# First MLP product token-major, convolution by accumulating transfers, gated result transposed: a two-layer encoder on one core

## The chip, the core and the metric

The program runs on one NeuronCore of a Trainium2 chip. The metric is device time of one execution in microseconds (us), a median of several runs. Engines are named as the profile names them: PE (TensorE: matmuls) and PEld (its weight loads), DVE (VectorE), ACT (ScalarE), POOL (GpSimd, here only a queue that issues transfers), SP (SyncE, the other queue of transfers).

## The reference

Two layers over 256 tokens of width 2048 (float32). Each layer has three sub-layers, and each of them adds its normed result to the residual stream:

1. token mixing: grouped-query attention beside a Fourier mix, merged by gates;
2. cross-attention into a memory of 256 tokens;
3. a gated MLP with a convolution over neighbouring tokens, the part that changes:

```python
def conv_ffn(h, w_up, conv_w, conv_b, w_down):
    u = h @ w_up                                    # 256 x 2048 by 2048 x 11264
    up = jnp.pad(u, ((0, 0), (1, 1), (0, 0)))
    u = up[:, :-2] * conv_w[0] + up[:, 1:-1] * conv_w[1] + up[:, 2:] * conv_w[2] + conv_b
    gate, val = u[..., :D_FF], u[..., D_FF:]        # D_FF = 5632
    return (jax.nn.gelu(gate, approximate=True) * val) @ w_down     # 5632 x 2048
```

`h` is the stream after an RMS norm, and the result is RMS-normed again before it is added.

## The kernel before

**Precision.** Every large product is done in three passes: both operands are split into a high part (a cast, on ACT, line 133) and a low part (what the cast lost, on DVE, line 134), and high x high, high x low and low x high are summed in PSUM. A weight unit (`Unit`) is 128 x 2048 values, loaded by SP in two halves of 512 KB into one of four slots (`w32`, line 112) and split into one of four buffer pairs (`whi`, `wlo`). So TensorE can be at most two units behind the split.

**Two ways to multiply.** *Token-major* (`mm_rows`, lines 301 to 303): the stationary operand is 128 tokens of the activations, the weights stream as 512 columns, three matmuls of 512 columns for a k tile and a half of the tokens, and the result has tokens on partitions. *Feature-major* (`block`, lines 151 and 152): the stationary operand is a 128 x 128 piece of the weights, the activations stream: 512 columns (high and low part of all 256 tokens) against the high weights, 256 columns against the low ones. The result has features on partitions and must be merged (`merge`, lines 223 and 224), as the first half of it holds high x high plus low x high, the second high x low.

**The MLP before.** Its first product is feature-major but for the first four chunks of 128 features, which are made token-major inside the sub-layer's boundary (`Columns`, weights `w_up_ko`) and turned by eight transposes (`ut`, line 1233). For every pair of chunks (gate and value, `up`, line 1208) the rows are merged, multiplied by the token's rstd, spread over all partitions by two small matmuls (`Pre.everywhere`), and convolved (`conv`, line 1189): with tokens along the free axis the neighbours are a shift of one element, so ACT does the own tap and the bias (line 1192) and DVE the left and the right one (lines 1195 and 1199). Then come GELU, the product (line 1224) and the split of the result into `G` (lines 228 and 229), which is at once the stationary operand of the second product. That goes in four quarters of 11 row tiles (`products`), one after every 11 (or 12, one ahead) chunk pairs; the first three quarters are added up in SBUF (`y`), the last goes into the boundary.

**What sets the order.** Tile, the layer that builds the program, puts in all semaphores. A planner simulates the program with its own prices and gives each engine a fixed order: of what is ready, the earliest in program order goes first. On the chip each engine and each queue keeps that order and waits in it. Only in `boundary` (line 458) is the order on DVE, ACT and PE written out by hand. The boundary takes the last part of one product (`steps`), renews the residual stream, transposes it into the next operand `A` and runs the first 512 columns of the next product (`cols`). `projected` (line 611) makes the four units of 512 columns of a token-major product as items, and `stream` (line 639) runs a list of items, prepares each one item ahead and calls `between` after every k tile.

Of the kernel before, what the change touches and what calls it, by code (L numbers as in the profile page):

```python
# [17 lines left out]
P = 128  # L18
D = 2048
# [7 lines left out]
NQ = 4  # L27
QK = DFF // P // NQ
# [8 lines left out]
O_BG, O_CW0, O_CW1, O_CW2, O_CB, NPAR = 112, 144, 232, 320, 408, 496  # L37
# [7 lines left out]
def encoder(ctx: ExitStack, tc: tile.TileContext, t, out):  # L45
# [325 lines left out]
    def products(src, S, nk, begin, finish, last, ahead=(), made=None, mid=None):  # L371
# [5 lines left out]
        for n in range(4):  # L377
            begin(n)
            pss = [psum(f"y{j}") for j in range(2)]
            split_at = nk  # L380
            if isinstance(last, tuple):
                split_at = 0 if n >= last[0] else nk
            elif n == 3:
                split_at = last
            for k0 in range(0, nk, 4):
                m = min(4, nk - k0)
                w = made or unit(src[n][:, k0 * 512 : (k0 + m) * 512], m * 512)
                made = None
                if k0 == 0 and n in ahead:
                    ahead[n]()  # L390
                for k in range(k0, k0 + m):
                    if k >= split_at:
                        late.append((n, pss, k, w, (k - k0) * 512))
                        continue
                    for j in range(2):
                        mm_rows(pss[j], S, k, j, w, (k - k0) * 512, k == 0, k == nk - 1)
            if split_at == nk:
                for j in range(2):
                    finish(j, n, pss[j])
            yield n  # L400
        for j in range(2):
            for i, (n, pss, k, w, col) in enumerate(late):
                mm_rows(pss[j], S, k, j, w, col, k == 0, k == nk - 1)
                if k == nk - 1:
                    finish(j, n, pss[j])
# [307 lines left out]
    for l in range(L):  # L713
# [448 lines left out]
        cols = Columns(t["w_up_ko"][l], A)  # L1162

        def ahead_apart(y, cols, tags):
# [12 lines left out]
            return {1: lambda: prepare(0), 2: lambda: prepare(1), 3: lambda: sqrt_ahead(y.ss[:, 0, 0:1])}  # L1177

        steps = products(t["w_xo"][l], OX, 4, y.gain, taken, (2,), ahead_apart(y, cols, "B"), w_first)
        for n in range(4):  # L1180
            next(steps)
        ss = boundary(y, steps, par[:, O_FFNPRE : O_FFNPRE + KT], A, cols)
        ut = tmp2("ut"), tmp2("ut")
        ut = [u.rearrange("p a n -> p (a n)") for u in ut]
        for j in range(2):
            nc.scalar.copy(ut[j], cols.ps[j])


        def conv(u, c, name):
            nc.vector.tensor_mul(u, u, pre.b)  # L1190
            r = tmp1(name)
            nc.scalar.activation(
                r, u, AF.Identity, scale=par[:, O_CW1 + c : O_CW1 + c + 1], bias=par[:, O_CB + c : O_CB + c + 1]
            )
            nc.vector.scalar_tensor_tensor(
                out=r[:, 1:T], in0=u[:, 0 : T - 1], scalar=par[:, O_CW0 + c : O_CW0 + c + 1], in1=r[:, 1:T],
                op0=ALU.mult, op1=ALU.add,
            )
            nc.vector.scalar_tensor_tensor(
                out=r[:, 0 : T - 1], in0=u[:, 1:T], scalar=par[:, O_CW2 + c : O_CW2 + c + 1], in1=r[:, 0 : T - 1],  # L1200
                op0=ALU.mult, op1=ALU.add,
            )
            return r

        NC = DFF // P
        G = [None] * NQ

        def up(c):

            qt, i = divmod(c, QK)  # L1210
            if i == 0:
# [29 lines left out]
        for qt in range(NQ):  # L1241
            until = min(NC, (qt + 1) * QK + (AHEAD if qt + 1 < NQ else 0))
            for c in range(done, until):
                up(c)
# [184 lines left out]
```

## Time and profile before

| | us |
|---|---|
| median of 3 runs (2913.4 to 2914.52) | 2914.01 |
| the profiled execution | 2912.27 |
| its span, first to last instruction | 2910.5 |
| PE busy in the span | 2897.6 |
| DVE busy | 2053.4 |
| ACT busy | 1583.6 |
| PE on line 151, the feature-major product's high weights, share of the chain | 21.5% |
| PE on line 152, its low weights | 11.0% |

The profile is one execution. A group's row gives line, engine, operation, tile written <- tiles read, shape, count, then busy time, mean ns of one, and idle time of the engine ahead of it. Matmuls overlap, and their drawn ends are modelled, so their price is read from start to start. The chain of waits follows the work that ended last back to its beginning. In the list of transfers the last column is the median time from issue to landing. A row of stretches gives, for each engine, busy time and count, then the clock granted to TensorE, the mean busy share of the 16 DMA engines and GB/s.

### The profile page before, as it was taken

To read this page: it belongs to the slowest core of one execution; us is meant where nothing else is said; L and a number is where in the kernel's file an instruction comes from. 1 tells how busy PE (TensorE), PEld (TensorE's weight loads), DVE (VectorE), ACT (ScalarE), POOL (GpSimd) and SP (SyncE) were. 2 spreads that over 40 slices of the span, in tenths; PEclk is the share of its full clock that TensorE was granted. 3 is DMA by queue.
4 is the path that set the end of the run, shared out by engine and by line. 5 is a ranking of instruction groups with operands and counts; after the bars stand their busy time and mean duration, and the time that the engine had idled before them with its cause. 6 is when DMAs were issued, how large, how long until landed. Compare 5 with 4: busy or idle time off the path is not lost.

```text
span 2910.5 us, 39133 instructions
## 1 busy us (share of the span) xinstructions
PE 2897.6 (100%) x14476; PEld 2443.7 (84%) x14476; DVE 2053.4 (71%) x2930; ACT 1583.6 (54%) x2479; POOL 34.9 (1%) x60
## 2 busy tenths in 40 slices
PE   9999999999999999999999999999999999999998
PEld 7888888888888888888878888888888888888887
DVE  6668767666875867767776587776678768677676
ACT  6556455555655545545555564445566555455454
POOL 0000000000000000000000000000000000000000
PEclk9999999999999999999999999999999999999999
DMA  8644776765666566565655456677556666666655
GB/s 290 188 148 159 232 235 224 226 187 160 196 184 195 187 188 191 180 200 184 212 174 182 145 163 222 222 236 215 181 159 202 187 193 186 188 190 186 195 185 163
DMA packets 161775, 563.09 MB, mean 193 GB/s; under 512 B 18480, under 2 KB 19504, under 8 KB 161584
## 3 DMA queue, kind: packets, MB, share of 16 engines
q1 hardware_dynamic: 156816, 545.53, 59.5%
q0 software_dynamic: 4480, 14.68, 1.8%
q8 instruction: 113, 1.85, 0.3%
q14 instruction: 78, 0.64, 0.1%
q10 hardware_dynamic: 288, 0.39, 0.0%
HBM read 556.34 MB, written 4.19 MB: 193 GB/s over the span
## 4 chain that ended last, share of the span: by engine, by line
PE 97%; DVE 1%; ACT 1%; DMA 0%; issue 0%; DVEq 0%; ACTq 0%
PE up L151 22%; PE up L152 11%; PE y L302 8%; PE y L303 8%; PE y L301 8%; PE g L301 4%; PE g L303 4%; PE g L302 4%; PE qk L302 3%; PE qk L303 3%; PE qk L301 2%; PE a L301 2%; PE a L303 2%; PE a L302 2%; PE as L302 2%; PE as L301 2%
## 5 line engine op out<-in xcount | busy, mean ns | idle before, releaser
L134 DVE TENSOR_TENSOR wlo<-w,whi 128x1024 fp32r<-128x1024 f32 (+1 forms) x981 | 1179.9, 1205 | 656.4 <-ACT whi L133 649.4
L133 ACT CAST whi<-w 128x1024 fp32r<-128x1024 f32 (+1 forms) x981 | 1015.6, 1037 | 955.6 <-PE y L303 295.4
L151 PE MATMUL up<-A_ff,whi 128*128 128x512 f32 x2688 | 946.3, 397 | 0.0
L152 PE MATMUL up<-A_ff,wlo 128*128 128x256 f32 x2688 | 755.0, 281 | 0.0
L151 PEld LDWEIGHTS up<-A_ff,whi 128*128 128x128 f32 x2688 | 504.9, 188 | 121.9
L152 PEld LDWEIGHTS up<-A_ff,wlo 128*128 128x128 f32 x2688 | 509.0, 189 | 0.4
L301 PE MATMUL y<-whi,G 128*128 128x512 f32 x704 | 274.3, 390 | 0.0
L302 PE MATMUL y<-wlo,G 128*128 128x512 f32 x704 | 274.2, 389 | 0.0
L303 PE MATMUL y<-whi,G 128*128 128x512 f32 x704 | 274.2, 389 | 0.0
L301 PE MATMUL g<-whi,A_mix 128*128 128x512 f32 x512 | 202.3, 395 | 0.0
L302 PE MATMUL g<-wlo,A_mix 128*128 128x512 f32 x512 | 200.8, 392 | 0.0
L303 PE MATMUL g<-whi,A_mix 128*128 128x512 f32 x512 | 200.3, 391 | 0.0
L303 PEld LDWEIGHTS y<-whi,G 128*128 128x128 f32 x704 | 132.2, 188 | 27.5
L301 PEld LDWEIGHTS y<-whi,G 128*128 128x128 f32 x704 | 132.2, 188 | 27.4
L302 PEld LDWEIGHTS y<-wlo,G 128*128 128x128 f32 x704 | 132.2, 188 | 27.2
L303 PE MATMUL qk<-whi,A_mix 128*128 128x512 f32 x320 | 125.6, 392 | 0.0
L302 PE MATMUL qk<-wlo,A_mix 128*128 128x512 f32 x320 | 125.4, 392 | 0.0
L301 PE MATMUL qk<-whi,A_mix 128*128 128x512 f32 x320 | 124.9, 390 | 0.0
L223 ACT COPY t<-up 128x256 f32<-128x256 f32 x168 | 61.7, 367 | 102.8 <-DVE G L229 84.7
L303 PEld LDWEIGHTS g<-whi,A_mix 128*128 128x128 f32 x512 | 96.3, 188 | 19.1
L301 PEld LDWEIGHTS g<-whi,A_mix 128*128 128x128 f32 x512 | 96.3, 188 | 18.4
L302 PEld LDWEIGHTS g<-wlo,A_mix 128*128 128x128 f32 x512 | 96.4, 188 | 17.9
(264 smaller groups left out, 4076.7 us busy)
## 6 DMA issues: line engine op xcount, KB each, us to landing
w<-in_w_up SPq DMA_DIRECT2D x336, 512.0 KB, 4.5
w<-in_w_dn SPq DMA_DIRECT2D x160, 512.0 KB, 4.0
w<-in_w_g SPq DMA_DIRECT2D x128, 512.0 KB, 4.3
w<-in_w_qk SPq DMA_DIRECT2D x80, 512.0 KB, 4.5
w<-in_w_ao SPq DMA_DIRECT2D x64, 512.0 KB, 5.0
w<-in_w_mo SPq DMA_DIRECT2D x64, 512.0 KB, 4.3
w<-in_w_vu SPq DMA_DIRECT2D x47, 512.0 KB, 4.5
w<-in_w_fo SPq DMA_DIRECT2D x32, 512.0 KB, 4.1
```

The costliest lines, as they stand in the source:

```text
L133: nc.scalar.copy(hi[:, :m], w[:, :m])
L134: nc.vector.tensor_sub(lo[:, :m], w[:, :m], hi[:, :m].bitcast(F32))
L151: nc.tensor.matmul(ps, hi, a, start=first, stop=False, skip_group_check=True)
L152: nc.tensor.matmul(ps[:, :T], lo, a[:, 0:T], start=False, stop=last, skip_group_check=True)
L223: nc.scalar.copy(b, ps[:, T : 2 * T])
L301: nc.tensor.matmul(ps, ah, hi, start=first, stop=False)
L302: nc.tensor.matmul(ps, ah, lo, start=False, stop=False)
L303: nc.tensor.matmul(ps, al, hi, start=False, stop=last)
```

## The change

The first product is token-major throughout: 22 *halves* of 512 features a layer (gate block, value block, gate block, ...), each in four units of four k tiles; the first half is the boundary's. With tokens on partitions, rstd is a scale for each partition (in the copy out of PSUM), and a neighbouring token is another partition or the other half of the tokens. So for each half DVE makes three products `u * tap` with taps that a transfer has spread over all partitions (768 KB on SP's queue), and the left and right ones are carried to the neighbour by transfers from POOL's queue which add into a sum that the bias (also spread, 2 x 256 KB from POOL) has been written to: 127 partitions of 4 KB, and one row of 2 KB, each way. Then DVE adds the sum to the own product. A value half is multiplied by the gate half, transposed on TensorE in groups of four 128 x 128 blocks and split into `G`.

Each step has a due number: the k tile after which it stands in the program, counted from the half's last matmul: product for the right 1, for the left 2, own 3, sum 11, GELU or gated product 12, transposes 13 and 14. The second product goes in parts of 16, 16 and 12 row tiles. The first two stand in the stream as items behind the gate half that follows their last block; the third is `products`, where the first two column blocks run over the first 8 row tiles ahead of their last 4.

```diff
-    def products(src, S, nk, begin, finish, last, ahead=(), made=None, mid=None):
+    def products(src, S, nk, begin, finish, last, ahead=(), made=None, mid=None, first=None, beside=None):
...
+        order = [(n, k0) for n in range(4) for k0 in range(0, nk, 4)]
+        if first is not None:
+            order.sort(key=lambda u: (u[0] > 1, u[0] < 2 and u[1] >= first, u))
+        pss = {}
+        for n, k0 in order:
+            if n not in pss:
+                begin(n)
+                pss[n] = [psum(f"y{j}") for j in range(2)]
...
+                for j in range(2):
+                    mm_rows(pss[n][j], S, k, j, w, (k - k0) * 512, k == 0, k == nk - 1)
+                if beside is not None:
+                    beside()
...
-        cols = Columns(t["w_up_ko"][l], A)
+        cols = Columns(t["w_up"][l, 0], A)
...
-            return {1: lambda: prepare(0), 2: lambda: prepare(1), 3: lambda: sqrt_ahead(y.ss[:, 0, 0:1])}
+            def prepare_last():
+                if n == 2:
+                    prepare(1)
+                sqrt_ahead(y.ss[:, 0, 0:1])
+
+            ahead = {n: lambda: prepare(0), 3: prepare_last}
+            if n == 1:
+                ahead[2] = lambda: prepare(1)
+            return ahead
...
+        def beside(i=None):
+
+            now = [f for n, f in due if n == 1]
+            due[:] = [(n - 1, f) for n, f in due if n > 1]
+            for f in now:
+                f()
+
+        def bias_of(h):
+
+            src = t["conv"][l, 3, h * 512 : (h + 1) * 512].partition_broadcast(P)
+            for j in range(2):
+                nc.gpsimd.dma_start(places["sum"][:, j], src)
+
+        def taps(i):
+
+            if not places:
+                c, d = [big.tile([P, 8, 512], F32, tag=tag, name=name) for tag, name in (("C", "cv"), ("D", "uv"))]
+                places.update(taps=(c[:, 0:3], c[:, 3:6]), sum=c[:, 6:8], gate=d[:, 0:2], val=d[:, 2:4])
+                places.update(left=d[:, 4:6], right=d[:, 6:8])
+                bias_of(0)
+            b, w = divmod(i, 2)
+            h = b + w * NB
+            to = places["taps"][w]
+            nc.sync.dma_start(to, t["conv"][l, 0:3, h * 512 : (h + 1) * 512].partition_broadcast(P))
+            return to
+
+        def half(i):
+
+            b, w = divmod(i, 2)
...
+            def finish(j, ps, to):
+                u = places["val" if w else "gate"]
+                nc.scalar.activation(u[:, j], ps, AF.Copy, scale=pre.t[:, j : j + 1])
+                if not j:
+                    return
+                s, left, right = [places[n] for n in ("sum", "left", "right")]
...
+                def give_right():
+                    nc.vector.tensor_mul(left, u, factor(0))
+                    nc.gpsimd.dma_start(s[1:P], left[0 : P - 1], accum_op=ALU.add)
+                    nc.gpsimd.dma_start(s[0:1, 1], left[P - 1 : P, 0], accum_op=ALU.add)
+
+                def give_left():
+                    nc.vector.tensor_mul(right, u, factor(2))
+                    nc.gpsimd.dma_start(s[0 : P - 1], right[1:P], accum_op=ALU.add)
+                    nc.gpsimd.dma_start(s[P - 1 : P, 0], right[0:1, 1], accum_op=ALU.add)
+
+                def own():
+                    nc.vector.tensor_mul(u, u, factor(1))
+
+                def together():
+                    nc.vector.tensor_add(u, u, s)
+                    if i + 1 < 2 * NB:
+                        bias_of((i + 1) // 2 + (i + 1) % 2 * NB)
+
+                def activate():
+                    if w:
+                        nc.vector.tensor_mul(u, u, places["gate"])
+                    else:
+                        nc.scalar.activation(u, u, AF.Gelu_apprx_tanh)
+
+                due.extend([(1, give_right), (2, give_left), (3, own), (11, together), (12, activate)])
+                if w:
+                    due.extend([(13, lambda: turn(0)), (14, lambda: turn(1))])
+
+            def turn(j):
+                q, k = divmod(b, DN)
+                if G[q] is None:
+                    G[q] = big.tile([P, 4 * min(DN, NB - q * DN), 2, T], F32R, tag="B", name="G")
+                pt = ps_sc.tile([P, 4, P], F32, tag="sc", name="gt")
+                for m in range(4):
+                    nc.tensor.transpose(pt[:, m], places["val"][:, j, m * P : (m + 1) * P], ident)
+                hi, lo = [G[q][:, 4 * k : 4 * k + 4, part, j * P : (j + 1) * P] for part in range(2)]
+                nc.scalar.copy(hi, pt)
+                nc.vector.tensor_sub(lo, pt, hi.bitcast(F32))
...
+        items = []
+        for i in range(1, 2 * NB):
+            items += up(i)
+            b = i // 2
+            if i % 2 == 0 and b % DN == 0:
+                q = b // DN - 1
+                for n in range(4):
+                    src = down(q, n)
+                    items += projected([src[:, u * UW : (u + 1) * UW] for u in range(4)], Down(q), "y", sum_down(q, n))
+        items.append(First())
+        ss = boundary(y, steps, par[:, O_FFNPRE : O_FFNPRE + KT], A, cols, then=items[0].make)
+        pre.of_squares(ss)
+        take = half(0)
+        factors = taps(0)
         for j in range(2):
-            nc.scalar.copy(ut[j], cols.ps[j])
-
-        def conv(u, c, name):
-            nc.vector.tensor_mul(u, u, pre.b)
...
+            take(j, cols.ps[j], factors)
+        y = Out(t["gpost"][l, 2])
+        for _ in stream(items, beside):
+            pass
...
+        steps = products(
+            [down(2, n) for n in range(4)], Down(2), 4 * (NB - 2 * DN), y.gain, lambda j, n, ps: y.take(j, n, ps, True), 4,
+            before_last, items[-1].w, mid=5, first=8, beside=beside,
+        )
```

The old `conv`, `up` and the loop over quarters are removed; `NB` = 11 and `DN` = 4. The columns of parameters lose the gate bias and the convolution's taps, and the weights are laid out on the host to fit.

More of the change, by code (lines that the diff above doesn't have):

```diff
@@ L1180, in encoder @@
+            return ahead
+        steps = products(t["w_xo"][l], OX, 4, y.gain, taken, (2,), ahead_apart(y, cols, "B", 1), w_first)
         for n in range(4):
             next(steps)
-        ss = boundary(y, steps, par[:, O_FFNPRE : O_FFNPRE + KT], A, cols)
-        ut = tmp2("ut"), tmp2("ut")
-        ut = [u.rearrange("p a n -> p (a n)") for u in ut]
-        for j in range(2):
-            nc.scalar.copy(ut[j], cols.ps[j])
-        def conv(u, c, name):
[L1190 to L1203, printed above, removed]
@@ L1238, in encoder @@
-        AHEAD = 1
-        done = 0
-        y = None
[L1241 to L1244, printed above, removed]
-            done = until
-            if qt == 0:
-                y = Out(t["gpost"][l, 2])
-            more = qt == NQ - 1 and l + 1 < L
-            def first_or_more(j, n, ps, qt=qt):
-                if qt == 0:
-                    nc.scalar.copy(y.at(j, n), ps)
-                elif qt < NQ - 1:
-                    nc.vector.tensor_add(y.at(j, n), y.at(j, n), ps)
-                else:
-                    y.take(j, n, ps, True)
-            if more:
-                A = operand("A_mix")
-                cols = Columns(t["w_vu"][l + 1, 0], A)
-            if more:
-                before_last = ahead_apart(y, cols, "CD")
-            else:
-                before_last = {3: lambda y=y: sqrt_ahead(y.ss[:, 0, 0:1])}
-            end = qt == NQ - 1
-            steps = products(
-                t["w_dn"][l, qt], G[qt], QK, y.gain if end else lambda n: None, first_or_more, 4 if end else QK,
-                before_last if end else (), mid=5 if end else None,
-            )
-            for n in range(4):
-                next(steps)
-            if qt < NQ - 1:
-                run(steps)
@@ new lines, in up, with __init__, __getitem__, down @@
+        def up(i):
+            b, w = divmod(i, 2)
+            return projected(t["w_up"][l, b + w * NB], A, "up", half(i), lambda: taps(i))
+        class Down:
+            def __init__(self, q):
+                self.q = q
+            def __getitem__(self, key):
+                return G[self.q][key]
+        def down(q, n):
+            return t["w_dn"][l, n][:, q * DN * UW :]
+        def sum_down(q, n):
+            def finish(j, ps, row):
+                if q == 0:
+                    nc.scalar.copy(y.at(j, n), ps)
+                else:
+                    nc.vector.tensor_add(y.at(j, n), y.at(j, n), ps)
+            return finish
```

115 lines of the change are left out of this document (47 added, 68 removed).

## The prediction

> **What bounds the kernel now.** I read the busy shares first, then the chain of waits by line, then single instructions.
>
> ```profile
> span 2910.5 us, 39133 instructions
> PE 2897.6 (100%) x14476; PEld 2443.7 (84%) x14476; DVE 2053.4 (71%) x2930; ACT 1583.6 (54%) x2479; POOL 34.9 (1%) x60
> by line: PE up L151 21.5%; PE up L152 11.0%; PE y L302 7.6%; PE y L303 7.6%; PE y L301 7.6%; PE g L301 4.0%; PE g L303 4.0%; PE g L302 4.0%; PE qk L302 2.5%; PE qk L303 2.5%; PE qk L301 2.5%; PE a L301 2.0%; PE a L303 2.0%; PE a L302 2.0%;
> ```
>
> TensorE is busy in all of the span, and the chain that ended last is almost only matmuls. So the time is a sum of matmul prices, and a change counts by what it does to that sum and by the stalls it brings. The chain's shares also price the MLP's first product: 21.5% and 11.0% of 2910.5 us are 945.9 us for 2688 pairs of matmuls at L151 and L152 (counts below), so 352 ns for a pair.
>
> What a matmul costs is read from start to start, because the trace draws each one longer than its turn. The next rows are TensorE's order of time, where a stretch of the second product (L301 to L303) gives way to the first (L151, L152). Columns: start, length drawn, engine, line, operation.
>
> ```profile
> 900.29 0.39 PE L301 MATMUL y<-whi,G 128*128 128x512 f32 x1
> ...
> 910.49 0.39 PE L151 MATMUL up<-A_ff,whi 128*128 128x512 f32 x1
> 910.71 0.28 PE L152 MATMUL up<-A_ff,wlo 128*128 128x256 f32 x1
> 910.83 0.40 PE L151 MATMUL up<-A_ff,whi 128*128 128x512 f32 x1
> L151 PE MATMUL up<-A_ff,whi 128*128 128x512 f32 x2688 | 946.3, 397 | 0.0
> L152 PE MATMUL up<-A_ff,wlo 128*128 128x256 f32 x2688 | 755.0, 281 | 0.0
> L301 PE MATMUL g<-whi,A_mix 128*128 128x512 f32 x512 | 202.3, 395 | 0.0
> ```
>
> From 900.29 to 910.49 stand 45 matmuls (15 triples) of 512 columns: 226.7 ns each. For one k tile a triple serves 128 tokens and 512 outputs, a pair 256 tokens and 128 outputs, so two triples do the work of four pairs, with as many columns streamed (1536 a triple, 768 a pair). But the pair takes 352 ns where half a triple takes 340.
>
> **The change, part by part. TensorE first.** Before, 84 of the 88 column blocks of a layer go as pairs, after, 21 of 22 halves of 512 columns go as triples: 2 layers x 21 x 96 = 4032 matmuls x 226.7 ns = 914.1 us in place of 945.9, so **-31.8 us**. The block of 512 columns inside the boundary is token-major in both. The second product keeps its 44 row tiles and its triples (11+11+11+11 before, 16+16+12 after): 0.
>
> What is added on TensorE are transposes of the gated result, four of 128x128 for each 512 columns and each 128 tokens. The same step stands in the attention stage (tile mt):
>
> ```profile
> 308.12 0.40 PE L303 MATMUL g<-whi,A_mix 128*128 128x512 f32 x1
> 308.36 0.60 PE L983 MATMUL mt<-con,work 128*128 128x128 f32 x4
> 308.71 0.48 PE L301 MATMUL g<-whi,A_mix 128*128 128x512 f32 x1
> 309.03 0.40 PE L302 MATMUL g<-wlo,A_mix 128*128 128x512 f32 x1
> ...
> 743.89 1.03 PE L1233 MATMUL ut<-con,ut 128*128 128x128 f32 x8
> 744.76 0.61 PE L252 MATMUL ps_pre<-dg,ones 128*128 128x128 f32 x4
> 745.13 0.48 PE L151 MATMUL up<-A_ff,whi 128*128 128x512 f32 x1
> 745.44 0.28 PE L152 MATMUL up<-A_ff,wlo 128*128 128x256 f32 x1
> ```
>
> From the matmul at 308.12 to the second one behind the group at 309.03 are 0.91 us, less two turns of 0.227: a group of four costs 0.457 us. 11 blocks x 2 x 2 layers = 44 groups: **+20.1 us**. Taken away are the eight transposes of ut and the four small matmuls that spread rstd over all partitions: 743.89 to 745.13 and 0.08 us of the slower matmul behind them (0.31 for 0.23), 1.3 us a layer: **-2.6 us**.
>
> The sum on TensorE is -31.8 + 20.1 - 2.6 = **-14.3 us**.
>
> **DVE and ACT**, which the chain hardly has:
>
> ```profile
> L134 DVE TENSOR_TENSOR wlo<-w,whi 128x1024 fp32r<-128x1024 f32 (+1 forms) x981 | 1179.9, 1205 | 656.4 <-ACT whi L133 649.4
> L133 ACT CAST whi<-w 128x1024 fp32r<-128x1024 f32 (+1 forms) x981 | 1015.6, 1037 | 955.6 <-PE y L303 295.4
> L1199 DVE SCALAR_TENSOR_TENSOR t<-t,par 128x255 f32<-128x255 f32 x176 | 85.3, 484 | 6.2
> L1195 DVE SCALAR_TENSOR_TENSOR t<-t,par 128x255 f32<-128x255 f32 x176 | 84.3, 479 | 1.5 <-ACT t L1192 1.3
> L1190 DVE TENSOR_TENSOR t<-t,rb 128x256 f32<-128x256 f32 x176 | 74.1, 425 | 5.4
> L224 DVE TENSOR_TENSOR t<-up,t 128x256 f32<-128x256 f32 x168 | 70.7, 421 | 36.1 <-ACT t L223 35.7
> L1224 DVE TENSOR_TENSOR t<-t 128x256 f32<-128x256 f32 x88 | 37.4, 425 | 4.4 <-ACT t L1223 1.0
> L229 DVE TENSOR_TENSOR G<-t,G 128x256 fp32r<-128x256 f32 x88 | 36.8, 419 | 0.0
> L134 DVE TENSOR_TENSOR wlo<-w,whi 128x512 fp32r<-128x512 f32 x34 | 23.4, 690 | 20.6 <-ACT whi L133 20.5
> L789 ACT ACTIVATE kug<-u,rstd_t 128x512 f32<-128x512 f32 x8 | 5.3, 682 | 2.0 <-PE u L303 2.0
> ```
>
> The six lines of DVE's convolution, merge and split (L1199 to L229) are 388.6 us and go. In come, for each of 44 halves, three products and one sum of 128x1024, priced by the split's 1.22 us (214.7 us), 22 gated products (26.8) and 44 low parts of 128x512 at 0.69 (30.2): 271.7 us. DVE gets 117 us of air. ACT loses its four activations a chunk pair and gains 88 copies out of PSUM at 0.68 and a few more. Neither is on the path, so I count 0; the cover is that a unit (four k tiles, 24 matmuls, 5.44 us) needs only 2.44 us of DVE for its weights.
>
> **The transfers** are where it is decided. A half lasts 96 x 226.7 ns = 21.8 us. Beside its 4.19 MB of weights it now moves 786 KB of taps (on SP's queue, ahead of weights), 524 KB of bias, and 1.05 MB that is added into SBUF, for which the old sum is read too:
>
> ```profile
> w<-in_w_up SPq DMA_DIRECT2D x336, 512.0 KB, 4.5
> w<-in_w_dn SPq DMA_DIRECT2D x160, 512.0 KB, 4.0
> w<-in_w_dn SPq DMA_DIRECT2D x32, 256.0 KB, 2.7
> gb<-in_gpost POOLq DMA_DIRECT2D x24, 256.0 KB, 5.0
> rows<-mir POOLq DMA_DIRECT2D x8, 256.0 KB, 4.8
> q1 hardware_dynamic: 156816, 545.53, 59.5%
> GB/s 290 188 148 159 232 235 224 226 187 160 196 184 195 187 188 191 180 200 184 212 174 182 145 163 222 222 236 215 181 159 202 187 193 186 188 190 186 195 185 163
> ...
> 30.00:40.00 10.00, 10.00 (x46) 8.29 (x45) 4.42 (x5) 8.73 (x19) 0.00 (x0) 1.00 1.04 397
> 286.00:510.00 224.00, 224.00 (x1001) 185.45 (x1000) 158.91 (x182) 112.08 (x129) 8.18 (x12) 1.00 0.72 233
> 1100.00:1200.00 100.00, 100.00 (x569) 86.71 (x568) 78.34 (x121) 56.87 (x88) 0.00 (x0) 1.00 0.61 189
> ```
>
> With the old sum counted that is 7.6 MB in 21.8 us, 348 GB/s. In the stretch 1100 to 1200 it is 189 GB/s at a share of 0.61, which would put 348 past the engines' end; but in 30 to 40 us 397 GB/s went through with TensorE busy in all ten. I take the second, as it is a rate reached and not a share stretched: 0. Weights have four slots, each due again after 10.9 us, less 4.5 for landing and 2.3 for splitting: 4.1 us to spare, against 2.0 us that the taps put ahead of them (786 KB at 397 GB/s).
>
> Then **the chain of one half**, on GpSimd's queue: product for the right neighbour, transfer, its one-row remainder, transfer to the left (it overlaps the first, so its issue waits for that landing, and the queue with it), remainder, sum on DVE. With t = 0 at the half's last matmul: ACT has both copies out by 0.9 (the first began a triple earlier), the first product ends at 2.1, both transfers land at 2.2 + L + 0.3 + L, and the sum and, in a value half, the gated product end 2 x 1.22 later: 4.9 + 2L. If a weight split is in the way it is 1.2 more. TensorE reaches the transposes after 13 of 16 k tiles of six matmuls, 1.36 us each, at 17.7. So **L up to 6.4 us costs nothing** (5.8 at worst), and behind that each value half stalls TensorE by 2 (L - 6.4), 22 of them in all.
>
> The trace has no transfer that accumulates and none between partitions of SBUF. Bounds for L: below 4.0, a plain 512 KB landing by SP; nearest is rows<-mir, out of SBUF by GpSimd, 4.8 us for 256 KB; doubling the size costs 1.3 us (2.7 to 4.0 with w_dn), so 6.1; above 9.6, twice 4.8, if adding doubles all. I take 6.1 as nearest in queue and size: stall 0, with 0.3 us in hand. Gate halves have no transposes: there only DVE stands at the sum, with weight splits and then SP's loads queued behind it. A split is ready 2.3 us after its buffer comes free and used 8.2 us after (three half units), so 5.9 us of waiting cost nothing. The bias for the next half follows the sum (issued at about 17, landing 5.0 later at 22, needed at 21.8 + 2.2 = 24): hidden, by 2 us.
>
> The order of the last product (first two column blocks over 8 tiles, then their last four) gives the last half four units, 21.8 us, of cover, as elsewhere. The late part at the layer's end grows from 7 to 8 triples for each half of the tokens, moved and not added. The next layer's first weights are asked for later, but still 16 us ahead: 0.
>
> **Sum:** the profiled execution took 2912.27 us (span 2910.5 and 1.8 around it). 2912.27 - 14.3 = 2898.0. The median of the runs shown lies 1.74 above that execution, so **2899.7, say 2900 us**.
>
> **Rivals.** *The sums come late* (slower side). L is over 6.4 because the transfer reads, adds and writes while weights fill the engines. The planner that orders each engine's instructions puts the sum where it guesses the landing; DVE and TensorE keep that order and wait. For it: nothing in the trace adds, and the margin is small. Against it: 4.8 us is measured with 233 GB/s beside it (286 to 510). Price: 44 us for each us of L; from L = 6.7 it eats the 14.3 us, at 7.8 the time is 2962, at 9.6 it is 2900 + 141 = 3041.
>
> *One DMA engine for 127 partitions.* All transfers here have 128 partitions, so how 127 are shared out is not seen. On one engine, 127 packets at 59.5% x 16 x 2910.5 us / 156816 = 177 ns are 22.4 us, and 4.1 us of fixed time (4.8 less four packets) make 26.5; twice that, products, sum and bias are 61 us for a half of 21.8. 38 halves have no second product behind them: + 39 x 38 = 1480, so 4390 us. The Trainium skill, page "DMA: Bandwidth & Descriptors", section "Why a DMA increments its semaphore by 16 and not by 1", says just that: the engines used are the largest number up to 16 that divides the slowest dimension, one for 127 partitions; it adds that some direct copies from GpSimd are spread over 16 all the same. No run here shows which of the two an accumulating copy gets.
>
> *The triples run no faster than the pairs,* because the pair's extra 12 ns comes from what runs beside it and not from its shape. Against it: g's 1536 matmuls have transposes and DVE work beside them, and their three shares of 4.0% are 349 us, 227 ns each. Price: no 31.8, so 2912.3 + 17.5 + 1.7 = 2931.
>
> *The DMA engines are full* at the 290 GB/s of the page's first slice: 6.55 MB (the old sum not counted, as the profile counts) then take 22.6 us, 0.8 more a half, 42 x 0.8 = 34 us: 2934. Against it: the 397 GB/s above.
>
> **How the numbers follow.** Forecast 0.50 (own range 2893 to 2908: a few tenths of a us on 22 value halves), late sums 0.27, one engine 0.10, triples as slow as pairs 0.06, engines full 0.07. The range 2890 to 2965 holds the forecast, two thirds of the late sums (up to L = 7.8) and the two small rivals, 0.79 together. About 0.2% (5.8 us) is what this kernel's runs can tell from no change. Faster: the forecast and 0.03 of barely late sums, 0.53. Same: late sums near L = 6.6 and half-true small rivals, 0.10. Slower: 0.37.
>
> **What would show it.** Triples of up at 0.227 from start to start; groups of four transposes at 0.45; TensorE with no idle time ahead of the transposes or of up's matmuls; accumulating transfers landing in 5 to 6.4 us. Wrong it is if DVE's sum shows long waits for a DMA and TensorE's transposes wait for DVE, if one accumulating transfer takes over 20 us, or if ACT's weight copies wait for w's DMA in the MLP.

## The result, and the profile after

The changed kernel takes **3226.65 us** (median of 4 runs, 3215.26 to 3231.19) against 2914.23 us in the same comparison: ratio **1.1067, 95% interval [1.1038, 1.1096]**. The forecast was 2900 us with a range up to 2965; the time lies 262 us above that range, and the kernel is slower where it was to be a little faster. The profiled execution took 3225.67 us, 313.4 more than the one of before.

First the page of the kernel after: span, busy shares, TensorE's granted clock in 40 slices, the queue of POOL, the chain's shares by engine, and the transfers with the median time from issue to landing.

```profile
span 3223.9 us, 36080 instructions
...
PE 2976.3 (92%) x13284; PEld 2448.7 (76%) x13284; DVE 1926.5 (60%) x2264; ACT 1477.0 (46%) x2083; POOL 234.9 (7%) x324
...
PEclk9999999998989988998999999999989999999999
...
q0 software_dynamic: 27008, 83.73, 15.0%
...
PE 62%; DMA 24%; DVE 7%; issue 3%; ACT 3%; POOL 1%; DVEq 0%; SPq 0%; POOLq 0%; ACTq 0%
...
w<-in_w_up SPq DMA_DIRECT2D x352, 512.0 KB, 6.3
...
cv<-uv POOLq DMA_DIRECT2D x88, 508.0 KB, 8.6
```

TensorE's share falls from 100% to 92%, and the chain that was almost all matmuls now has 24% of DMA. The accumulating transfer lands in 8.6 us (forecast: 6.1), and the weights of the first product in 6.3 instead of 4.5. The slices of the clock that are not 9 (the row counts tenths of the full clock) lie in the two MLPs.

Next the waits of the kernel after: who waited for whom, us in total, times, longest.

```profile
DVE uv L1262 <- DMA cv<-uv: 469.3, 44, 14.0
...
POOL cv L1218 <- DVE uv L1262: 398.2, 41, 12.3
...
POOL cv L1256 <- DMA cv<-uv: 242.3, 34, 7.9
...
PE gt L1282 <- DVE uv L1268: 141.6, 22, 11.0
...
PE up L303 <- DVE wlo L135: 75.7, 18, 5.3
...
PE y L303 <- DVE wlo L135: 18.0, 4, 5.4
```

L1262 is the sum. VectorE stands in it in every one of the 44 halves, 10.7 us on average. TensorE then waits in two places. Behind the sum of each of the 22 value halves it waits before the transposes (L1282), for the gated product. Behind the sum of each of the 22 gate halves it waits before a matmul with low weights (L303), of the value half that it is then working on or, four times, of the second product (`y`): for a weight split that is queued behind the sum on VectorE.

One half, in the chain of waits of the kernel after (start, length, what; from the last matmuls of a gate half to TensorE at work again in the value half behind it):

```profile
925.55 0.24 PE up L304
...
925.82 1.38 ACT uv L1240 x2
...
927.22 1.24 DVE uv L1249
...
928.74 8.59 DMA cv<-uv
...
937.86 0.60 POOL cv L1256
938.46 8.92 DMA cv<-uv
...
947.70 0.06 DVE uv L1262
...
948.85 1.23 DVE wlo L135
...
950.12 0.80 PE up L303
950.91 0.43 PE up L304
951.34 0.43 PE up L302
...
954.75 0.35 PE up L304
955.10 0.23 PE up L302
```

From the half's last matmul (it ends at 925.8) to the landing of the second transfer (947.4) are 21.6 us: a whole half's matmuls are 21.8. And when TensorE goes on at 950, its matmuls of 512 columns take 0.43 us instead of 0.23 until 954.7. What VectorE does in that time shows in its timeline:

```profile
935.74 1.23 DVE L135 TENSOR_TENSOR wlo<-w,whi 128x1024 fp32r<-128x1024 f32 x1 [1.49 <-ACT whi L134]
947.70 1.23 DVE L1262 TENSOR_TENSOR uv<-uv,cv 128x1024 f32<-128x1024 f32 x1 [10.73 <-DMA cv<-uv]
948.85 1.22 DVE L135 TENSOR_TENSOR wlo<-w,whi 128x1024 fp32r<-128x1024 f32 x1
```

The sum stands 10.73 us ahead of its data, and the split that TensorE needs at 950 stands behind it.

**Where the 313 us are.** Taken from start to start, the MLPs' matmuls last 1426.8 us before and 1740.7 after (+313.9); everything else is unchanged. Of the kernel after: 22 gaps before transposes 145.1 us; 22 gaps behind the sums of gate halves 97.2; 283 matmuls at half rate behind the gaps (0.43 us) +56.5; 41 matmuls that come first behind a gap or a group of transposes, 0.57 or 0.59 us each, +14.4; the transposes themselves at half rate +12.9 (28.4 us for 44 groups, against 15.6 with no transfers, in the first run below). Without these 326.1 us the matmuls would be 12.2 us shorter than before.

### The profile page after: what moved, and what is told of

It reads as the page before. It is cut to its first block, busy times and chain, and to the rows that moved or that the text cites. A ratio compares the mean times of both kernels' runs of the same rounds, so it can differ in the third digit from the quotient of the medians.

```text
span 3223.9 us, 36080 instructions
## 1 busy us (share of the span) xinstructions
PE 2976.3 (92%) x13284; PEld 2448.7 (76%) x13284; DVE 1926.5 (60%) x2264; ACT 1477.0 (46%) x2083; POOL 234.9 (7%) x324
## 4 chain that ended last, share of the span: by engine, by line
PE 62%; DMA 24%; DVE 7%; issue 3%; ACT 3%; POOL 1%; DVEq 0%; SPq 0%; POOLq 0%; ACTq 0%
DMA cv<-uv 22%; PE y L303 6%; PE y L304 6%; PE y L302 6%; PE g L302 4%; PE g L303 4%; PE g L304 4%; PE up L303 3%; PE up L304 3%; PE up L302 3%; PE qk L302 2%; PE qk L303 2%; PE qk L304 2%; PE a L304 2%; PE a L302 2%
## 5 line engine op out<-in xcount | busy, mean ns | idle before, releaser
L135 DVE TENSOR_TENSOR wlo<-w,whi 128x1024 fp32r<-128x1024 f32 (+1 forms) x965 | 1168.1, 1221 | 655.3 <-ACT whi L134 652.0
L303 PE MATMUL up<-wlo,A_ff 128*128 128x512 f32 x1344 | 548.5, 408 | 75.7 <-DVE wlo L135 75.7
L302 PE MATMUL up<-whi,A_ff 128*128 128x512 f32 x1344 | 550.5, 410 | 0.0
L304 PE MATMUL up<-whi,A_ff 128*128 128x512 f32 x1344 | 544.4, 405 | 0.0
L303 PEld LDWEIGHTS up<-wlo,A_ff 128*128 128x128 f32 x1344 | 266.8, 198 | 137.9 <-DVE wlo L135 83.3
L1262 DVE TENSOR_TENSOR uv<-uv,cv 128x1024 f32<-128x1024 f32 x44 | 53.9, 1225 | 469.3 <-DMA cv<-uv 469.3
L304 PEld LDWEIGHTS up<-whi,A_ff 128*128 128x128 f32 x1344 | 266.3, 198 | 57.6
L302 PEld LDWEIGHTS up<-whi,A_ff 128*128 128x128 f32 x1344 | 266.7, 198 | 55.2
L303 PE MATMUL y<-wlo,G 128*128 128x512 f32 x704 | 278.6, 396 | 18.0 <-DVE wlo L135 18.0
L302 PE MATMUL y<-whi,G 128*128 128x512 f32 x704 | 279.1, 396 | 0.0
L304 PE MATMUL y<-whi,G 128*128 128x512 f32 x704 | 278.3, 395 | 0.0
L303 PE MATMUL g<-wlo,A_mix 128*128 128x512 f32 x512 | 200.7, 392 | 0.0
L1282 PE MATMUL gt<-con,uv 128*128 128x128 f32 x176 | 42.4, 388 | 141.6 <-DVE uv L1268 141.6
L303 PEld LDWEIGHTS y<-wlo,G 128*128 128x128 f32 x704 | 135.0, 192 | 47.8 <-DVE wlo L135 19.7
L1282 PEld LDWEIGHTS gt<-con,uv 128*128 128x128 f32 x176 | 32.2, 207 | 156.4 <-issue 154.1
L304 PE MATMUL qk<-whi,A_mix 128*128 128x512 f32 x320 | 125.3, 392 | 0.0
L303 PE MATMUL qk<-wlo,A_mix 128*128 128x512 f32 x320 | 125.2, 391 | 0.0
```

What stands on the lines that cost most here:

```text
L135: nc.vector.tensor_sub(lo[:, :m], w[:, :m], hi[:, :m].bitcast(F32))
L302: nc.tensor.matmul(ps, ah, hi, start=first, stop=False)
L303: nc.tensor.matmul(ps, ah, lo, start=False, stop=False)
L304: nc.tensor.matmul(ps, al, hi, start=False, stop=last)
L1262: nc.vector.tensor_add(u, u, s)
L1282: nc.tensor.transpose(pt[:, m], places["val"][:, j, m * P : (m + 1) * P], ident)
```

## The experiments

**Theory:** the two transfers in a row, and what waits for them, cost the 313 us. **Rivals:** the bytes themselves, that is weights which come late because the transfers fill the DMA engines; and the new matmuls and transposes.

**1. No transfers.** The four accumulating transfers of each half are left out, so the neighbours' share is missing from the sum; all other steps stay, bias and factors too. (With nothing to wait for, the planner moves the sum up: on VectorE it follows the own product at once in 40 of the 44 halves, where two weight splits stood between them in the kernel after. The same holds for the second run.)

```diff
-                    nc.gpsimd.dma_start(s[1:P], left[0 : P - 1], accum_op=ALU.add)
-                    nc.gpsimd.dma_start(s[0:1, 1], left[P - 1 : P, 0], accum_op=ALU.add)
...
-                    nc.gpsimd.dma_start(s[0 : P - 1], right[1:P], accum_op=ALU.add)
-                    nc.gpsimd.dma_start(s[P - 1 : P, 0], right[0:1, 1], accum_op=ALU.add)
```

> The four accumulating transfers of a half are left out, so the neighbours' taps are missing from the output; taps, bias, products, sum, transposes and their order in the program stay. Theory (the sum waits for the transfers, and TensorE waits for the sum and then runs at half its clock for a while): 3225.7 less the 242 us of stalls and about 80 us of slow matmuls behind them in the MLP, so about 2903, and at any rate 2890 to 2915. Rival (the triples, the transposes or the loads of taps and bias cost more than the sum allowed for): over 2940.

Measured: 2900.2 us, ratio 0.9953 [0.9936, 0.9969], 13.5 us below the kernel before. The matmuls are 12.8 us shorter than before, with no gap over 1 us. So the whole loss comes from the transfers and what waits for them, and nothing of it from the new matmuls.

**2. The same transfers, and nobody waits.** They add into a tile that nobody reads, so again the neighbours' share is missing.

```diff
+                away = t1[:, 0:4].rearrange("p (j a) n -> p j (a n)", j=2)
...
-                    nc.gpsimd.dma_start(s[1:P], left[0 : P - 1], accum_op=ALU.add)
+                    nc.gpsimd.dma_start(away[1:P], left[0 : P - 1], accum_op=ALU.add)
```

(and the other three alike)

> All transfers stay, with the same bytes, the same queue and the same waits among them, but they add into a tile that nobody reads; the sum reads the bias alone, so the neighbours' taps are missing from the output. Theory (waiting is what costs): 2900 to 2930, with stalls of TensorE under 20 us. Rival (the load on the DMA engines costs, weights land in 6.3 us instead of 4.5): 3050 or more, with ACT still waiting for weights.

Measured: 2922.2 us, ratio 1.0037 [1.0023, 1.005]. The load alone costs 22 us over the first run, the waiting the other 304. The waits of the first run and then of this one show where the 22 go: ScalarE, which makes the high part of the weights, waits longer for them.

```profile
ACT whi L134 <- DMA w<-in_w_up: 85.2, 37, 4.1
```

```profile
ACT whi L134 <- DMA w<-in_w_up: 312.1, 173, 6.2
```

**3. Two ways to a shorter landing.** First the same transfers as plain copies into the same tile (they overwrite the sum instead of adding to it, so the bias and one neighbour are lost); then 128 partitions in place and no remainder rows (no shift, so each token gets its own value for its neighbours').

```diff
-                    nc.gpsimd.dma_start(s[1:P], left[0 : P - 1], accum_op=ALU.add)
+                    nc.gpsimd.dma_start(s[1:P], left[0 : P - 1])
```

```diff
-                    nc.gpsimd.dma_start(s[1:P], left[0 : P - 1], accum_op=ALU.add)
-                    nc.gpsimd.dma_start(s[0:1, 1], left[P - 1 : P, 0], accum_op=ALU.add)
+                    nc.gpsimd.dma_start(s, left, accum_op=ALU.add)
```

> The four transfers of a half overwrite instead of adding, so the sums are wrong; bytes written, partitions, queue and waits stay. If adding is what makes a transfer long (it reads the old sum too, and its packets take 328 ns where a plain one takes 159), the landing falls from 8.6 to about 6 us and the time to 2950 to 3080. If the shift by a partition, the 127 rows or the queue make it long, the landing stays over 7.8 us and the time over 3150.

> Each half has two accumulating transfers of all 128 partitions onto the same partitions instead of the shifted 127 and the two rows; the neighbours' taps land on the own token. If 127 partitions are shared out badly over the DMA engines, the landing falls below 6.5 us and the time below 3050. If adding itself or the queue sets it, the landing stays at 7.8 us or more; two issues fewer take 1 to 2 us off each half, so 3100 to 3200.

Measured, one execution each: 3141.08 and 3187.32 us. Landing of the first and of the second transfer, in the answers on their lines (fewest, median, most us): plain copies, then 128 partitions.

```profile
DMA to landing us min/median/max: 4.2/5.8/8.3
...
DMA to landing us min/median/max: 6.2/10.3/12.2
```

```profile
DMA to landing us min/median/max: 5.6/6.4/9.8
...
DMA to landing us min/median/max: 5.2/8.2/9.9
```

In the kernel after they are 8.4 and 9.1. Not adding takes 2.6 us off the first and nothing off the second, which runs beside the next half's 768 KB of factors (that this makes it long is not shown); 16.1 us for the pair still puts the sum too late. The adding costs engine time as well: the POOL queue's share is 10.9% of 3139.3 us here against 15.0% of 3223.9 us for the same packets, a difference of 2260 us of engine time, so 0.2 us for each of the 11176 packets that add. What follows: not adding is worth 85 us of the 313, and two in a row are too long in both forms. The 39 us of the second run price its form less well: there the planner put the sum one weight split earlier than in the kernel after, and all of TensorE's 44 gaps stand before matmuls that need a weight split, none before transposes.

**4. Place against loop.** Two explanations of the waits were left: VectorE stands in the sum too early (its place), or the one sum tile makes a loop that is longer than a half (bias in, first transfer, second, sum, next bias). The first run moves the sum, and with it what follows it, four steps later and ties it behind every weight split made so far: five or six splits stand ahead of it now instead of two. The second run also gives gate and value a sum tile each.

```diff
-                    nc.vector.tensor_add(u, u, s)
+                    with tc.issue_after(Unit.made.ins):
+                        nc.vector.tensor_add(u, u, s)
...
-                due.extend([(1, give_right), (2, give_left), (3, own), (11, together), (12, activate)])
+                n = 11 if i + 1 == 2 * NB else 15
+                due.extend([(1, give_right), (2, give_left), (3, own), (n, together), (n + 1, activate)])
...
-                    due.extend([(13, lambda: turn(0)), (14, lambda: turn(1))])
+                    due.extend([(n + 2, lambda: turn(0)), (n + 3, lambda: turn(1))])
```

```diff
-                nc.gpsimd.dma_start(places["sum"][:, j], src)
+                nc.gpsimd.dma_start(places["sum"][h // NB][:, j], src)
...
-                    if i + 1 < 2 * NB:
-                        bias_of((i + 1) // 2 + (i + 1) % 2 * NB)
+                    if i + 2 < 2 * NB:
+                        bias_of(b + 1 + w * NB)
```

> The whole computation. The sum stands four steps later and behind all weight splits that are made before it, so that VectorE waits in it with no split behind it that TensorE needs soon; the four accumulating transfers and the one sum tile stay. Theory A (what costs is where VectorE stands waiting): the transfers are in place 21.6 us after the half's last matmul, the sum now begins at about 20, so nearly all of the stalls go: 2915 to 2960 us. Theory B (the loop of the one sum tile: bias row in 5.1 us, first transfer 8.6, second 8.9, two issues of 1, sum 1.2 and 1 of waits make 25.8 us, against 21.8 us for the matmuls of a half): each of 44 halves still takes 4 us more, 3080 to 3130 us.

> The whole computation. As the run with the later sum, and with a sum tile of its own for the gate and for the value, whose bias is fetched a whole half ahead. Theory A: no better than the run with the later sum alone, both 2915 to 2960 us. Theory B: the loop is gone, and only the transfers' load is left (2922 with nobody waiting): 2920 to 2960 us, at least 120 us below the run with the later sum alone.

Measured: 3115.75 us, 1.0696 [1.0674, 1.0717], and 3017.9 us, 1.036 [1.0339, 1.0381]. Both explanations hold in part. With the place alone the gaps behind the gate halves' sums are gone (97.2 to 8.2 us), 111 us in all; but the loop stays, as theory B had it. The chain of that run shows one turn of it, from sum to sum:

```profile
796.17 1.24 DVE uv L1263
...
797.70 0.60 POOL cv L1218
798.30 5.08 DMA cv<-in_conv
...
803.97 7.50 DMA cv<-uv
...
812.00 0.49 POOL cv L1256
812.49 11.07 DMA cv<-uv
...
823.85 1.24 DVE uv L1263
```

27.7 us, against 21.8 us of matmuls. In 17 of the 44 halves it was the bias that the first transfer waited for last, 92.8 us together (answer on its line, L1250). A second sum tile takes 98 us more off. I had expected 120 or more and a time near 2940; what is left are mainly the gaps before the transposes, seen in the waits with one sum tile and then with two:

```profile
PE gt L1284 <- DVE uv L1269: 160.5, 22, 11.5
```

```profile
PE gt L1286 <- DVE uv L1271: 82.1, 22, 6.6
```

**5. The two shifts side by side.** The rows from the left go as a plain copy into a tile of their own, which is added too; with the sum where the planner wants it, and then three steps later and tied.

```diff
-                    nc.gpsimd.dma_start(s[0 : P - 1], right[1:P], accum_op=ALU.add)
-                    nc.gpsimd.dma_start(s[P - 1 : P, 0], right[0:1, 1], accum_op=ALU.add)
+                    nc.gpsimd.dma_start(places["other"][0 : P - 1], right[1:P])
+                    nc.gpsimd.dma_start(places["other"][P - 1 : P, 0], right[0:1, 1])
...
+                    nc.vector.tensor_add(u, u, places["other"])
```

> The whole computation. The rows from the left go beside those from the right, as a plain copy into a tile of their own, with one more addition on VectorE (44 times 1.2 us, of which VectorE has room); places and order of the sum as they were. The chain from product to sum is then one accumulating transfer (8.6) instead of two (17.5), in place about 4.9 + 1 + 8.6 = 14.5 us after the half's last matmul, and the loop of the sum tile falls from 25.8 to some 18 us. If two transfers in a row are the cause: 2905 to 2940 us, ratio 0.997 to 1.009. If it is the accumulating form or the load of the queues and not the row of two, the second copy is as late as before: above 3050 us.

> The whole computation. The rows from the left beside those from the right, and the sum three steps later, behind the weight splits. If the one transfer of 8.6 us already comes in time with the sum where it was, this equals the run before it within 6 us; if VectorE's place still costs, it is 10 to 40 us faster than that. The floor is 2900 (no transfers) plus up to 22 for the load: 2905 to 2925 us.

Measured: 3147.66 us, 1.0813 [1.0792, 1.0834], and 3090.63 us, 1.0613 [1.0595, 1.0631]. I expected some 2920 for both; that was wrong, and the later, tied sum is worth 57 us. The answer on the copy's line in the first of them, and TensorE's wait there:

```profile
L1258 POOL DMA_DIRECT2D t<-uv x44: 564/566/1188, 753.5 to 3068.5; - x44
...
DMA to landing us min/median/max: 9.7/10.5/13.2
```

```profile
PE up L303 <- DVE wlo L135: 115.1, 38, 8.8
```

Side by side a transfer takes longer (the copy 10.5 us and the accumulating one 9.3, against 5.8 for the first of two copies in a row), and the planner put the first of the two additions one weight split earlier than the sum of the kernel after, so this run is not the clean test of the chain that I meant it to be. In the second run the gaps before transposes are back (137.2 us by start-to-start times, 37.9 in the first): the sum is tied behind splits of the matmuls that follow, and these come late. In the half whose transposes start at 956.7 us, for one, the sum stands behind a split whose weights landed after 13.25 us. So the tie has a price of its own.

**6. Late transposes, then copies alone.** First: two sum tiles, the tie, the sum one step later still, and the transposes at 22 and 23 instead of 17 and 18 (the GELU's result gets a place of its own). Second: no accumulating transfer at all. Both shifts are plain copies into two tiles, VectorE adds both and the bias, which is now fetched once per half (256 KB) and spread over both halves of the tokens when it is read; sum, product and transposes are due at 14, 16 and 20 here, where the first of the two has 16, 18 and 22.

```diff
-                due.extend([(1, give_right), (2, give_left), (3, own), (11, together), (12, activate)])
+                a, b_, c = (11, 12, 13) if i + 1 == 2 * NB else (16, 18, 22)
+                due.extend([(1, give_right), (2, give_left), (3, own), (a, together), (b_, activate)])
...
-                    due.extend([(13, lambda: turn(0)), (14, lambda: turn(1))])
+                    due.extend([(c, lambda: turn(0)), (c + 1, lambda: turn(1))])
```

```diff
+            places["bias"] = tmp2("bias").rearrange("p a n -> p (a n)")
+            nc.gpsimd.dma_start(places["bias"], src)
...
+                    nc.gpsimd.dma_start(s[1:P], left[0 : P - 1])
...
+                    nc.gpsimd.dma_start(places["other"][0 : P - 1], right[1:P])
...
                     nc.vector.tensor_mul(u, u, factor(1))
+                    nc.vector.tensor_add(u, u, places["bias"].unsqueeze(1).to_broadcast([P, 2, 512]))
...
+                        nc.vector.tensor_add(u, u, s)
+                        nc.vector.tensor_add(u, u, places["other"])
```

> The whole computation. Two sum tiles and the later sum, and besides the transposes eight steps (11 us) later in TensorE's order, which needs a place of its own for the GELU's result. With two sum tiles alone, 3018, the sums were in time for all but the transposes, before which TensorE stood 92.7 us in 22 gaps and ran 16 us slower after them. If the chain of two transfers is harmless once everything that waits for it stands late enough, those 109 us go too, but for one gap per layer at the last half: 2915 to 2935 us (2922 was the time with nobody waiting). If the load of the transfers makes the weights late as soon as nothing stretches a half, it stays above 2945.

> The whole computation. Both shifts as plain copies side by side into tiles of their own, no accumulating transfer; the bias row once instead of twice per half (256 KB less), added on VectorE; two more additions on VectorE per half (44 times 2.4 us, beside TensorE); sum and transposes late. If the accumulating packets (328 ns against 159) carry the load's 22 us, half of it goes or more: 2902 to 2912 us, just below the time before (ratio 0.996 to 1.000). If the load is that of the bytes, it equals the run with late transposes within 6 us.

Measured: 3000.37 us, 1.0297 [1.028, 1.0314], and 2947.96 us, 1.0122 [1.0105, 1.0139]. The late transposes won 18 us, not the hundred I expected. The gaps moved: they now stand before weights, the last line of the waits of the first of the two.

```profile
ACT whi L134 <- DMA w<-in_w_up: 369.8, 162, 6.2
...
PE up L303 <- DVE wlo L135: 38.9, 30, 4.6
```

The second run took off 52 us more, by copies instead of additions and by its earlier due numbers together; on VectorE the sum stands behind five splits in both. I had allowed either 2902 to 2912 or no change, and it was neither. VectorE's timeline of that run shows what was left:

```profile
875.47 1.23 DVE L135 TENSOR_TENSOR wlo<-w,whi 128x1024 fp32r<-128x1024 f32 x1 [0.56 <-ACT whi L134]
879.46 1.23 DVE L135 TENSOR_TENSOR wlo<-w,whi 128x1024 fp32r<-128x1024 f32 x1 [2.76 <-ACT whi L134]
880.60 1.22 DVE L1270 TENSOR_TENSOR uv<-uv,cv 128x1024 f32<-128x1024 f32 x1
```

The copies, issued at 863.0 and 865.3, land after 4.4 and 7.9 us (medians), so by 874. But the sum (L1270) is tied behind a split that waits for weights until 879.5.

**7. The sum before that split.** Sum at step 12 instead of 14, GELU or product at 13, transposes at 24 and 25 (the two diffs are against the run before each); then the same with the factors in three transfers of 256 KB between the weights' loads.

```diff
-                a, b_, c = (11, 12, 13) if i + 1 == 2 * NB else (14, 16, 20)
+                a, b_, c = (11, 12, 13) if i + 1 == 2 * NB else (12, 13, 24)
```

```diff
-            nc.sync.dma_start(to, t["conv"][l, 0:3, h * 512 : (h + 1) * 512].partition_broadcast(P))
+            def tap(k):
+                nc.sync.dma_start(to[:, k], t["conv"][l, k, h * 512 : (h + 1) * 512].partition_broadcast(P))
+
+            for k in range(3):
+                if i:
+                    due.append((2 + 3 * k, lambda k=k: tap(k)))
+                else:
+                    tap(k)
```

> The whole computation. Two plain copies as in the run before, with the sum two steps earlier and the transposes four later. There the copies were in place 14.7 us after the half's last matmul, but the sum stood behind a weight split that came at 20, and TensorE stood 21.7 us in 14 gaps before the transposes and 18 us in gaps of half a microsecond. If only these places were left, 2905 to 2920 us, ratio 0.998 to 1.003. If the load of the copies sets the rest (weights that land late), it stays above 2930.

> The whole computation. As the run before, and the convolution's 768 KB of factors per half in three transfers of 256 KB, three steps apart between the weights' loads, instead of one ahead of them on the same queue. If late weights are what is left (ScalarE waited 321 us for them with two copies, 85 with no transfer at all), this is 5 to 15 us faster than the run before: 2898 to 2912 us. If not, it equals it within 4 us.

Measured: **2904.55 us, ratio 0.9974 [0.9964, 0.9984]**, a little faster than the kernel before and far faster than the one after; and 2929.27 us, 1.0053 [1.004, 1.0067]. The first is as expected. Its page and its waits:

```profile
span 2902.2 us, 36098 instructions
...
PE 2886.5 (99%) x13284; PEld 2389.4 (82%) x13284; DVE 2032.6 (70%) x2378; ACT 1476.5 (51%) x2105; POOL 149.9 (5%) x280
```

```profile
ACT whi L134 <- DMA w<-in_w_up: 220.1, 107, 6.7
```

TensorE is at 99% again, with a single gap over 1 us in both MLPs. The copies land in 6.5 and 8.8 us here, longer than the 6.4 us that the forecast could bear, but they run side by side, and hardly anything stands where it has to wait for them. The matmuls last 1420.0 us, 6.8 less than before and 6.0 more than with no transfers. The second run missed by 25 us: ScalarE's wait for the weights of the first product goes up to 314.3 us. The weights' own landing does not change (5.9 us in the median against 6.0), so with three small loads spread between them ScalarE waits longer for another reason, which no run shows.

## Why the prediction was wrong, step by step

*TensorE's sum, -14.3 us: right.* With no transfers the time falls by 13.5 us. Its terms hold too: a group of four transposes, measured as the forecast did, costs 0.447 us in that run (19.7 us for 44 groups, forecast 20.1). Of this 0.354 us lie between the group's start and the next matmul, and most of the rest in that matmul, which is slower (0.31 us). All 6142 matmuls of 512 columns together last 5.4 us more than at 226.7 ns, some 4 us of it in those slower ones.

*DVE and ACT, 0: right.* Their busy time costs nothing: the kernel of the seventh experiment has 106 us more of VectorE work than the kernel after and is 322 us faster. It is VectorE's order that costs, not its load.

*"0" for the load of the transfers: wrong by 22 us,* the difference of the first two runs. I chose the row with 397 GB/s against the one with 0.61 of the engines' time at 189 GB/s. From 700 to 1560 us the kernel before has 0.61 and 188 GB/s, the run with nobody waiting 0.84 and 246. The rows of stretches say so (columns as in the prediction; the kernel before, then that run), and that run's list of transfers the landing of the weights:

```profile
700.00:1560.00 860.00, 858.65 (x4431) 728.96 (x4429) 623.83 (x902) 468.93 (x730) 4.29 (x8) 1.00 0.61 188
```

```profile
700.00:1560.00 860.00, 849.77 (x3777) 691.53 (x3776) 553.35 (x556) 406.32 (x515) 104.32 (x140) 1.00 0.84 246
...
w<-in_w_up SPq DMA_DIRECT2D x352, 512.0 KB, 7.5
```

The engines are not full on average, but the weights' landing goes from 4.5 to 7.5 us, 3.0 more, past the 2.1 us (4.1 to spare, less 2.0 for the taps) that I had counted. The rival of full engines priced this at 34 us.

*"I take 6.1 as nearest in queue and size: stall 0, with 0.3 us in hand": the step that failed.* The landing L is 8.4 us for the first transfer and 9.1 for the second, so the sum, which had 0.3 us in hand, comes late in every half. The bracket (4.0 to 9.6) held it; the choice inside it did not. It took the adding at nothing: without it the first lands in 5.8 us (experiment 3), with it in 8.4. And it took the second like the first: that one lands in 10.3 us without adding too, and why stays open. The formula's price at L = 8.75 is 22 x 2 x 2.35 = 103 us, so 3003.

*Most of the remaining 224 us were terms missing from the rival's price* of 44 us for each us of L. There are three, with what they measured:

- The gate halves, "there only DVE stands at the sum ... 5.9 us of waiting cost nothing". VectorE (DVE) waits 10.7 us there, as the planner put the sum that far ahead of its data. The price is 97.2 us; with the sum tied behind the splits it is 8.2.
- "The bias for the next half follows the sum ... hidden, by 2 us." True for a sum at 17, false for one at 22: then the bias, two transfers and the sum make a loop, 27.7 us in the turn shown of the run with the late sum, for a half of 21.8. A second tile is worth 98 us in the run with the late sum; in the kernel after, I take it, it hides in the gaps before the transposes, 145.1 us instead of 103; no run shows that part alone.
- The clock. Behind a gap TensorE runs at half rate: +83.8 us, with the transposes and the matmuls right behind them. The forecast had no term for that. Of the 44 gaps, the 42 of 3.6 us or more (here from one matmul's start to the next) were all followed by matmuls at 0.43 us, and the two of 2.0 and 2.5 us were not; in the run with two copies none of 16 gaps of 1.0 to 1.8 us was. The Trainium skill, page "TensorE: Matmul & The Clock Gate", section "Part 1: The HAM clock gate (the "warmup" mystery)", says that after an idle window of about 3.4 us the array gets every second clock and needs about as long of work to get all of it back. The trace agrees for the long gaps, those of 4 us or more in every run, with a median of 4.0 us at half rate behind the 42; from 1.8 to 3.9 us the runs show both.

*One DMA engine for 127 partitions: excluded.* 127 partitions land in 8.4 us and 128 in 6.4; one engine would need 127 x 0.2 = 25 us for the adding alone. So of the rule and the exception in the Trainium skill's page "DMA: Bandwidth & Descriptors", section "Why a DMA increments its semaphore by 16 and not by 1", accumulating copies from GpSimd follow the exception, with the packets spread. *Triples as slow as pairs: excluded* by the first run.

So the rival of late sums was the right one, with a chance of 0.27; at the measured L its price covers 103 of the 326 us of gaps and slow matmuls. Two slips in the forecast's sums change nothing: the chances inside its range add up to 0.81, not 0.79, and 2900 + 1480 us are 4380, not 4390.

## What to carry to other kernels

A transfer that replaces a shift inside an engine is to be priced as a chain and as a loop: from the product through every transfer that must follow another to the next use of the same tile. If it comes near the length of a stage, as 21.6 us did here beside 21.8, the engines wait for it, however little else they have to do. And a wait costs by its place in an engine's order: the same two shifts took 3227 us as two accumulations into one tile, and 2905 us as two copies into two tiles, with the sum placed between two weight splits where both its data and its followers had time. What the copies, the second tile and the place would each bring alone in that last kernel was not run. When stalls of several microseconds come in, add the half-rate stretch behind each of them.

## What the runs showed of the hardware that was not expected

- Adding costs a transfer inside SBUF about 0.2 us of engine time for each packet of 4 KB (from the queue's shares in experiment 3), and POOL 0.91 us for the issue instead of 0.55.
- A transfer inside SBUF has no landing time of its own: the same plain copy of 508 KB took 4.4 to 12.0 us in the medians of these runs (4.4 for the first of two in experiment 6, 12.0 in the second run of experiment 5), with different transfers beside it.
- Gaps well under 4 us can halve TensorE's clock too: in the run with nobody waiting, gaps of 1.76 and 1.26 us close together were followed by seven matmuls at 0.43 us, while in the run with two copies none of the 16 gaps of 1.0 to 1.8 us was followed by any.
- Splitting one broadcast load of 768 KB into three of 256 KB made the kernel 25 us slower: ScalarE waited 314.3 us for the first product's weights instead of 220.1, at the same landing. The cause stays open.
